# Narrow products of latent attention on whole 32-bit operands instead of split ones

## The chip, the core and the metric

The kernel runs on one core of a Trainium2 chip. A core has five engines with instruction queues of their own: TensorE (PE, the matrix engine; its weight loads are listed apart as PEld), VectorE (DVE), ScalarE (ACT), GpSimd (POOL) and SyncE (SP, which issues the transfers here). Each queue is worked in order, and the engines wait for each other through semaphores. Operands lie in an on-chip memory of 128 partitions, and matrix products land in banks of 512 32-bit words a partition. The metric is the time of one execution on the device in microseconds (us).

## The reference

A decoder trunk of two layers over 256 tokens of width 1024, all in 32-bit floats. Each layer is a half-step feed-forward part, an attention part, a second half-step feed-forward part and a gated input embedding, each followed by a layer norm. The first layer's attention is a forgetting attention; the second layer's is multi-head latent attention with 16 heads, and this is where the change lies:

```python
def scores(start):
    qn = lax.dynamic_slice_in_dim(q_nope, start, BLOCK_Q, axis=1)
    qr = lax.dynamic_slice_in_dim(q_rope, start, BLOCK_Q, axis=1)
    s = jnp.einsum('bqhd,bkhd->bhqk', qn, k_nope) + jnp.einsum('bqhr,bkr->bhqk', qr, k_rope)
    return s.astype(jnp.float32) * scale
...
    s = jnp.where(k_pos[None, :] <= q_pos[:, None], s, -jnp.inf)
    w = jax.nn.softmax(s, axis=-1).astype(v.dtype)
    return jnp.einsum('bhqk,bkhd->bqhd', w, v)
```

The attention is causal and swept over two blocks of 128 queries. The first block sees the first 128 keys alone, the second block all 256.

## The kernel before

**Split operands.** TensorE is used with a reduced 32-bit type (F32R). To keep the accuracy, every operand is split in two parts: a high part, which ScalarE makes by copying to F32R, and a low part, which VectorE makes by subtracting the high part from the original (`parts`, lines 520 to 524, for results in the product banks; `split`, lines 174 to 220, for weights that come from memory). A product is then three passes (`mm3`, lines 505 to 510): high by high, high by low, low by high. Transposes through TensorE (`transpose`, line 516) and the warm-up products of `spin` (line 489) are the only ones on whole 32-bit data.

**Weights.** `Stream` loads weights in groups into three raw buffers through SP and splits them into slots (`hl0` and so on, and lent tiles such as `qk`, `ota`, `otb`, `fs`). When a split is put into the program is decided while the program is written, from a simple count of each engine's time (`busy`, `pump`, `fill`, `ahead`). In the latent attention the turns at which `pump` may split are switched off for nearly the whole stage (`hold 1`), and the list `ORDER` (lines 48 to 75) says when splits are made: `f n` fills up to n weights ahead, `a` makes the high part of one split, `l` makes its low part.

**The latent attention** (`mla`, from line 1261). `ORDER` also fixes the order of the steps. For each head h:

- `gen h` multiplies the latents by the head's weights and leaves, in one bank, 256 columns of queries (two blocks of 128) and 256 columns of keys; `parts` splits all 512 columns into one half of the tile `qk` (even heads one half, odd heads the other).
- `QK h` makes the scores: block 0 by the first 128 keys (128 columns), block 1 by all 256 keys (256 columns). Each takes three passes on the split nope parts and two passes with the rope part (`zT` and `kr`; the trace names these `fs,xT`).
- `sm h` and `div h` do the softmax: mask and minimum on VectorE (line 1455), exponential on ScalarE (line 1460), scaling on VectorE (line 1472).
- `T h` transposes the 384 columns of probabilities in three pieces and splits them into the tile `PT`. Columns 0 to 255 belong to the first 128 keys (both query blocks), columns 256 to 383 to the second 128 keys (second query block alone).
- `AV h` multiplies by the values: three passes of 256 columns for the first 128 keys, three of 128 columns for the second 128 keys, then `parts` into an output tile. `O h t` is the output projection.

The values are made four heads at a time: `V g t` (group g of four heads, key block t) leaves a bank of 512 columns and copies its high part on ScalarE; `vlo g t` later makes the low part on VectorE and lets the bank go. Values live in a ring of five buffers named `g4`.

Scores and transposes share two banks called `tr`; `gen` and `AV` share two called `h`. `rope copy`, `rot`, `zs` and `zU` prepare the rope part of heads 8 to 15 in the early part of the stage, partly on GpSimd.

Of the kernel before, what the change touches and what calls it, by code (L numbers as in the profile page):

```python
# [10 lines left out]
F32 = mybir.dt.float32  # L11
F32R = mybir.dt.float32r
AF = mybir.ActivationFunctionType
# [409 lines left out]
class Trunk:  # L423
# [837 lines left out]
    def mla(self, li):  # L1261
        nc, S, a = self.nc, self.S, self.a
# [4 lines left out]
        v = {}  # L1267
        cqt = self.tl([128, 2, 3, 256], F32R, "gb", 1)
        cqtok = self.tl([128, 2, 768], F32, "PT", 1)
        zt = self.own([128, 2, D], F32, "ota")  # L1270
        qk = self.own([128, 2, 2, 512], F32R, "qk")

        dqb, dqr = {}, {}
# [20 lines left out]
        vps = {}  # L1294

        def V(g, t):
            w = self.use(("kvv", g))
            ps = vps[g, t] = self.bank(("h", "y", "tr")[VRING[g][t]])
            for k in range(2):
                self.mm3(  # L1300
                    ps, lambda i: self.ckv[:, i, 256 * k + 128 * t : 256 * k + 128 * t + 128],
                    lambda i: w[:, i, 512 * k : 512 * k + 512], k == 0, k == 1,
                )
            o = v[t, g] = self.tl([128, 2, 512], F32R, "g4", 5)
            nc.scalar.activation(o[:, 0, :], ps, AF.Copy)
            S.busy(act=512)
# [107 lines left out]
        st, PT = {}, {}  # L1414

        def gen(h):
            ps = self.bank("h")
            hp, s = h // 2, h % 2
            w = self.use(("kvk", hp))
            for k in range(2):  # L1420
                self.mm3(
                    ps[:, 256:512], lambda i: w[:, i, 256 * k + 128 * s : 256 * k + 128 * s + 128],
                    lambda i: self.ckv[:, i, 256 * k : 256 * k + 256], k == 0, k == 1,
                )
            w = self.use(("qn", hp))
            for k in range(3):
                self.mm3(
                    ps[:, 0:256], lambda i: w[:, i, 256 * k + 128 * s : 256 * k + 128 * s + 128],
                    lambda i: cqt[:, i, k, :], k == 0, k == 2,
                )  # L1430
            o = qk[:, h % 2]
            self.parts(o[:, 0, :], o[:, 1, :], ps)

        def QK(h):
            b = self.bank("tr")
            kr = self.kr
            o = qk[:, h % 2]
            for q0, c0, c1 in ((0, 0, 128), (128, 128, 384)):
                w = c1 - c0
                self.mm3(  # L1440
                    b[:, c0:c1], lambda i: o[:, i, q0 : q0 + 128],
                    lambda i: o[:, i, 256 : 256 + w], True, False,
                )
                for i in (0, 1 + (h % 2 if h < 8 else 1)):
                    self.mm(b[:, c0:c1], zT[:, h, q0 : q0 + 128], kr[:, i, 0:w], False, i > 0)
            st[h] = b
# [34 lines left out]
        def T(h):  # L1481
# [4 lines left out]
            o = self.tl([128, 2, 384], F32R, "PT", 1)  # L1486
            self.parts(o[:, 0, :], o[:, 1, :], b[:, 0:384])
            PT[h] = o

# [7 lines left out]
        def AV(h):  # L1497
            if h in (0, 10):
                OT.append(self.own([128, 4, 2, 256], F32R, "ota" if h else "otb"))
            o = PT.pop(h)  # L1500
            ps = self.bank("h")
            g, c = h // 4, 128 * (h % 4)
            for m, (i, jj) in enumerate(((0, 0), (0, 1), (1, 0))):
                self.mm(
                    ps[:, 0:256], v[0, g][:, i, c : c + 128], o[:, jj, 0:256], m == 0, False
                )
            for m, (i, jj) in enumerate(((0, 0), (0, 1), (1, 0))):
                self.mm(
                    ps[:, 128:256], v[1, g][:, i, c : c + 128], o[:, jj, 256:384], False, m == 2
                )  # L1510
            ot = ot_of(h)
# [107 lines left out]
```

## Time and profile before

| What | Value |
|---|---|
| Time, median of 3 runs | 1083.85 us (1083.05 to 1084.26) |
| Profiled execution, span from first to last instruction | 1080.8 us |
| Median of the runs less that span | 3.05 us |
| TensorE busy | 1065.8 us, 99% of the span |
| VectorE busy | 718.8 us, 67% |
| ScalarE busy | 543.3 us, 50% |
| Transfers over the span | 183 GB/s |

The profile gives no time of the profiled execution beside its span; what lies around the span is taken from the median of the runs. In a row of the groups, a line of the kernel, an engine and an operation are followed by the written and read tiles, the shape and the count; after the bar stand the busy time in us and the mean of one in ns, and after the second bar the idle time of the engine just before them, with what ended it. In the timeline a row begins with its start and length in us, and neighbours of one kind are merged. Matrix passes overlap in the records, so their pitch from start to start tells more than their length. A waits row gives the waiting engine and line, what ended the wait, the total in us, how often, and the longest.

### The profile page before, as it was taken

The page shows a single profiled execution, that of the slowest core. Times are in us where ns is not written, and L with a number is a line of the kernel's source. Part 1 is how long each engine was busy: PE and PEld are TensorE (multiplying, and loading weights), DVE is VectorE, ACT ScalarE, POOL GpSimd, SP SyncE. Part 2 cuts the span into 40 slices and gives each one's busy share as a digit, 9 for nine tenths or more (in the row PEclk, how much of TensorE's full clock was granted, in tenths as well). Part 3 has the DMA queues.
Part 4 walks back from the last instruction along what each step waited for, and adds up shares of the span by engine and source line. Part 5 has one row for each costly group of instructions (what it writes and reads, how often), then busy time and mean ns, then how long its engine had stood idle before and what let it go on. Part 6 is the DMA issues. An engine that isn't in the chain of part 4 may idle for free.

```text
span 1080.8 us, 17731 instructions
## 1 busy us (share of the span) xinstructions
PE 1065.8 (99%) x7210; PEld 971.2 (90%) x7210; DVE 718.8 (67%) x1042; ACT 543.3 (50%) x806; POOL 73.2 (7%) x104
## 2 busy tenths in 40 slices
PE   9999999999999999999999999999999999999996
PEld 7989999899879999998899999988899889898986
DVE  4665645888797545558966564388777886455566
ACT  4565433666646444444555443336576465444431
POOL 0000000222200000000320000012200000000000
PEclk9999999999999999999999999999999999999999
DMA  8787752653358756455588564343445568565502
GB/s 270 230 312 241 245 181 83 195 166 137 114 172 290 254 181 190 148 201 156 164 275 266 185 194 165 89 105 112 140 145 169 174 225 308 191 206 192 182 13 78
DMA packets 151428, 198.54 MB, mean 184 GB/s; under 512 B 11954, under 2 KB 130994, under 8 KB 151348
## 3 DMA queue, kind: packets, MB, share of 16 engines
q1 hardware_dynamic: 151348, 197.43, 55.8%
q8 instruction: 56, 0.92, 0.3%
q14 instruction: 24, 0.20, 0.1%
HBM read 196.35 MB, written 1.05 MB: 183 GB/s over the span
## 4 chain that ended last, share of the span: by engine, by line
PE 90%; DVE 6%; issue 2%; ACT 2%; POOL 1%; DVEq 0%; POOLq 0%; ACTq 0%
PE y L513 32%; PE h L513 32%; PE tr L513 23%; PE tr L517 2%; DVE hl L195 2%; DVE x L593 1%; ACT hl L194 1%; DVE st L575 0%; DVE x L574 0%; PE h L517 0%; DVE PT L523 0%; ACT P L1460 0%; PE tr L1100 0%; DVE g L833 0%; POOL rs L585 0%
## 5 line engine op out<-in xcount | busy, mean ns | idle before, releaser
L195 DVE TENSOR_TENSOR hl<-raw,hl 128x1024 fp32r<-128x1024 f32 (+3 forms) x276 | 321.4, 1183 | 152.0 <-ACT hl L194 150.4
L194 ACT ACTIVATE hl<-raw 128x1024 fp32r<-128x1024 f32 (+3 forms) x276 | 274.4, 1016 | 187.0 <-PE y L513 95.0
L513 PE MATMUL y<-hl,g 128*128 128x512 f32 x816 | 190.7, 390 | 0.0
L513 PEld LDWEIGHTS y<-hl,g 128*128 128x128 f32 x816 | 152.0, 188 | 30.7
L513 PE MATMUL tr<-xT,hl 128*128 128x256 f32 x1512 | 177.3, 277 | 0.0
L513 PEld LDWEIGHTS tr<-xT,hl 128*128 128x128 f32 x1512 | 174.6, 188 | 0.9 <-DVE hl L195 0.2
L513 PE MATMUL h<-xT,hl 128*128 128x256 f32 x1464 | 174.0, 278 | 0.1
L513 PEld LDWEIGHTS h<-xT,hl 128*128 128x128 f32 x1464 | 170.0, 188 | 1.5 <-DVE qk L523 0.3
L513 PE MATMUL h<-hl,xT 128*128 128x512 f32 (+2 forms) x348 | 80.9, 379 | 0.5 <-DVE xT L523 0.4
L513 PEld LDWEIGHTS h<-hl,xT 128*128 128x128 f32 x348 | 61.5, 188 | 13.0 <-DVE xT L523 0.9
L513 PE MATMUL y<-hl,xT 128*128 128x512 f32 (+3 forms) x360 | 65.4, 334 | 0.0
L513 PEld LDWEIGHTS y<-hl,xT 128*128 128x128 f32 x360 | 55.5, 188 | 6.3 <-ACT xT L522 0.4
L585 POOL TENSOR_TENSOR rs<-ve,mhalf 128x1 f32<-128x1 f32 x16 | 15.2, 952 | 601.2 <-DVE ve L584 601.2
L522 ACT ACTIVATE xT<-tr 128x512 fp32r<-128x512 f32 (+1 forms) x36 | 19.2, 550 | 57.1 <-PE tr L517 57.0
L513 PE MATMUL y<-hl,otb 128*128 128x512 f32 x168 | 43.4, 399 | 0.7 <-DVE hl L195 0.5
L523 DVE TENSOR_TENSOR g<-P,g 128x512 fp32r<-128x512 f32 x37 | 25.6, 692 | 25.8 <-ACT g L522 25.8
L522 ACT ACTIVATE g<-P 128x512 fp32r<-128x512 f32 x37 | 23.4, 632 | 32.2 <-DVE P L708 32.2
L513 PEld LDWEIGHTS y<-hl,otb 128*128 128x128 f32 x168 | 30.2, 188 | 7.2 <-DVE hl L195 0.8
L195 DVE TENSOR_TENSOR otb<-raw,otb 128x1024 fp32r<-128x1024 f32 (+1 forms) x20 | 24.1, 1202 | 16.8 <-ACT otb L194 16.8
L195 DVE TENSOR_TENSOR qk<-raw,qk 128x1024 fp32r<-128x1024 f32 (+1 forms) x21 | 25.7, 1222 | 10.8 <-ACT qk L194 10.8
L707 ACT ACTIVATE P<-tr 128x512 f32<-128x512 f32 x20 | 12.0, 598 | 40.2 <-PE tr L513 40.2
L708 DVE TENSOR_TENSOR P<-P,tr 128x512 f32<-128x512 f32 x20 | 13.8, 688 | 26.8 <-PE tr L513 15.1
(259 smaller groups left out, 1411.6 us busy)
## 6 DMA issues: line engine op xcount, KB each, us to landing
raw<-in_ffn_w_in_dram SPq DMA_DIRECT2D x170, 512.0 KB, 4.8
raw<-in_ffn_w_out_dram SPq DMA_DIRECT2D x44, 1024.0 KB, 5.0
raw<-in_fox_w_in_dram SPq DMA_DIRECT2D x11, 1024.0 KB, 5.4
raw<-in_ple_w_gate_dram SPq DMA_DIRECT2D x8, 1024.0 KB, 5.1
raw<-in_mla_w_o_dram SPq DMA_DIRECT2D x8, 1024.0 KB, 5.0
gb<-in_ln_g_dram SPq DMA_DIRECT2D x8, 512.0 KB, 6.4
gb<-in_ln_b_dram SPq DMA_DIRECT2D x8, 512.0 KB, 7.8
raw<-in_fox_w_o_dram SPq DMA_DIRECT2D x4, 1024.0 KB, 4.9
```

Of the source, the lines that this page charges most:

```text
L194: nc.scalar.activation(hi[:, c], src[:, c], AF.Copy)
L195: nc.vector.tensor_tensor(lo[:, c], src[:, c], hi[:, c].bitcast(F32), op=ALU.subtract)
L513: self.nc.tensor.matmul(out, lhsT, rhs, start=start, stop=stop)
L517: self.nc.tensor.transpose(out, in_, self.ident)
L522: self.nc.scalar.activation(hi, src, AF.Copy)
L523: self.nc.vector.tensor_tensor(lo, src, hi.bitcast(F32), op=ALU.subtract)
L585: nc.gpsimd.tensor_tensor(rs, ve, self.mhalf, op=ALU.pow)
L593: nc.vector.scalar_tensor_tensor(xs, xs, rs if i else mv[:, 0:1], self.gb[:, i, c0:c1], op0=ALU.mult if i else ALU.subtract, op1=ALU.add i ...
L707: nc.scalar.activation(gt, ps[0], AF.Silu)
L708: nc.vector.tensor_tensor(gt, gt, ps[1], op=ALU.mult)
```

## The change

Two of the four products of a head, both 128 columns wide, are made on the whole 32-bit operands, in one call each instead of three passes on the split parts: the scores of query block 0 (`QK`), and the values of the second 128 keys (`AV`).

- `gen` splits only columns 128 to 511 (384 instead of 512) and copies the first 128 queries and the first 128 keys unsplit to a raw place (one more ScalarE copy of 256 columns, read with a stride). `heads(h)` names these places. The query block 0 is no longer kept split.
- `T` splits 256 columns instead of 384 and copies the last 128 unsplit (one more ScalarE copy of 128 columns).
- `V g 1` copies its bank unsplit; the four steps `vlo g 1` are gone from `ORDER`, and nothing else of that list is changed.
- The raw places are tiles under names that earlier parts of the kernel have done with: `negc` (the raw queries and keys of even heads in columns 0 to 255, and the raw probabilities of all heads in columns 256 to 383) and `nrm` (odd heads), the latter taken in `gen 1`.

```diff
         qk = self.own([128, 2, 2, 512], F32R, "qk")
+        raws = [self.tl([128, 384], F32, "negc", 1)]
...
-            o = v[t, g] = self.tl([128, 2, 512], F32R, "g4", 5)
-            nc.scalar.activation(o[:, 0, :], ps, AF.Copy)
+            if t:
+                o = v[t, g] = self.tl([128, 512], F32, "g4", 5)
+                nc.scalar.activation(o, vps.pop((g, t)), AF.Copy)
+            else:
+                o = v[t, g] = self.tl([128, 2, 512], F32R, "g4", 5)
+                nc.scalar.activation(o[:, 0, :], ps, AF.Copy)
...
+        def heads(h):
+            return qk[:, h % 2, :, 0:384], raws[h % 2][:, 0:256]
+
         def gen(h):
...
-            o = qk[:, h % 2]
-            self.parts(o[:, 0, :], o[:, 1, :], ps)
+            if h == 1:
+                raws.append(self.tl([128, 384], F32, "nrm", 1))
+            o, raw = heads(h)
+            self.parts(o[:, 0, :], o[:, 1, :], ps[:, 128:512])
+            nc.scalar.activation(
+                raw.rearrange("p (i c) -> p i c", i=2), ps.rearrange("p (i c) -> p i c", i=2)[:, :, 0:128], AF.Copy)
+            S.busy(act=256)
 
         def QK(h):
...
-                self.mm3(
-                    b[:, c0:c1], lambda i: o[:, i, q0 : q0 + 128],
-                    lambda i: o[:, i, 256 : 256 + w], True, False,
-                )
+                if q0:
+                    self.mm3(b[:, c0:c1], lambda i: o[:, i, 0:128], lambda i: o[:, i, 128:384], True, False)
+                else:
+                    self.mm(b[:, c0:c1], raw[:, 0:128], raw[:, 128:256], True, False)
+                    S.busy(pe=128)
...
             o = self.tl([128, 2, 384], F32R, "PT", 1)
-            self.parts(o[:, 0, :], o[:, 1, :], b[:, 0:384])
-            PT[h] = o
+            raw = raws[0][:, 256:384]
+            self.parts(o[:, 0, 0:256], o[:, 1, 0:256], b[:, 0:256])
+            nc.scalar.activation(raw, b[:, 256:384], AF.Copy)
+            S.busy(act=128)
+            PT[h] = o, raw
...
-            for m, (i, jj) in enumerate(((0, 0), (0, 1), (1, 0))):
-                self.mm(
-                    ps[:, 128:256], v[1, g][:, i, c : c + 128], o[:, jj, 256:384], False, m == 2
-                )
+            self.mm(ps[:, 128:256], v[1, g][:, c : c + 128], raw, False, True)
+            S.busy(pe=128)
```

More of the change, by code (lines that the diff above doesn't have):

```diff
@@ L1436, in QK @@
             kr = self.kr
-            o = qk[:, h % 2]
+            o, raw = heads(h)
             for q0, c0, c1 in ((0, 0, 128), (128, 128, 384)):
                 w = c1 - c0
-                self.mm3(
-                    b[:, c0:c1], lambda i: o[:, i, q0 : q0 + 128],
-                    lambda i: o[:, i, 256 : 256 + w], True, False,
-                )
+                if q0:
[3 more added lines that the diff above has]
+                    S.busy(pe=128)
                 for i in (0, 1 + (h % 2 if h < 8 else 1)):
@@ L1499, in AV @@
                 OT.append(self.own([128, 4, 2, 256], F32R, "ota" if h else "otb"))
-            o = PT.pop(h)
+            o, raw = PT.pop(h)
             ps = self.bank("h")
```

8 rows, old and new, of the table ORDER are left out of this document.

## The prediction

> **What bounds the kernel now.** I read the page first (busy time by engine, the chain that ended last), then the groups by line and shape, then the timeline of the attention stage.
>
> ```profile
> span 1080.8 us, 17731 instructions
> PE 1065.8 (99%) x7210; PEld 971.2 (90%) x7210; DVE 718.8 (67%) x1042; ACT 543.3 (50%) x806; POOL 73.2 (7%) x104
> PE 90%; DVE 6%; issue 2%; ACT 2%; POOL 1%; DVEq 0%; POOLq 0%; ACTq 0%
> ```
>
> TensorE (PE) is busy 99% of the span and is 90% of the last chain. Work taken off PE shortens the run, except where PE was going to wait anyway. The next view gives those waits between 690 and 880 us, around the attention stage, and the one after 850 us.
>
> ```profile
> PE h L513 <- DVE hl L195: 1.6, 2, 1.0
> PE tr L517 <- ACT qk L522: 1.1, 1, 1.1
> PE y L513 <- DVE hl L195: 0.5, 1, 0.5
> PE h L513 <- DVE PT L523: 0.4, 1, 0.4
> PE tr L517 <- DVE P L1472: 0.4, 1, 0.4
> ```
>
> ```profile
> PE tr L517 <- DVE x L593: 0.2, 1, 0.2
> ```
>
> So about 4 us of waiting in the stage, nearly all for a weight split or a probability on VectorE (DVE). By stretches (columns: length; busy PE, PEld, DVE, ACT, POOL with counts; granted clock; DMA share; GB/s) it lies early:
>
> ```profile
> 740.00:760.00 20.00, 16.51 (x116) 14.56 (x115) 16.71 (x33) 11.48 (x25) 10.82 (x9) 1.00 0.28 86
> 760.00:780.00 20.00, 19.91 (x130) 17.72 (x130) 14.47 (x38) 12.91 (x33) 2.10 (x2) 1.00 0.46 139
> 800.00:820.00 20.00, 20.00 (x142) 18.61 (x141) 16.16 (x39) 13.27 (x31) 0.00 (x0) 1.00 0.52 165
> ```
>
> From 760 us PE has no room left, and a saved PE nanosecond counts in full; from 740 to 760 us others set the pace. The granted clock is 1.00 throughout.
>
> **The products.** Here is the first head's scores step, its passes merged by kind: three of 128 columns on the split nope parts, two of 128 with the rope part, then three and two of 256, then the next head.
>
> ```profile
> 741.01 0.45 PE L513 MATMUL tr<-qk 128*128 128x128 f32 x3
> 741.30 0.39 PE L513 MATMUL tr<-fs,xT 128*128 128x128 f32 x2
> 741.52 0.57 PE L513 MATMUL tr<-qk 128*128 128x256 f32 x3
> 741.92 0.40 PE L513 MATMUL tr<-fs,xT 128*128 128x256 f32 x2
> 742.16 0.45 PE L513 MATMUL tr<-qk 128*128 128x128 f32 x3
> ```
>
> From start to start the ten passes take 742.16 - 741.01 = 1.15 us, 0.115 each, although five of them stream half as many columns. A 128-column pass is thus not cheaper than a 256-column one: within 1.15 us the rope pair of 256 takes 0.24, so 0.120 each. Each pass brings its own weight load, and a narrow pass is held to the pitch of these. Removing a pass saves a slot, some 0.11 us.
>
> The only products on whole 32-bit operands in this trace are the warm-up ones of line 493, 384 columns wide. The second-last and last of their matrix records (merged, then the last alone), the load beside the former, and from the page a load of split operands:
>
> ```profile
> 5.64 0.81 PE L493 MATMUL y<-mask 128*128 128x384 f32 x2
> 5.96 0.49 PE L493 MATMUL y<-mask 128*128 128x384 f32 x1
> 5.64 0.19 PEld L493 LDWEIGHTS y<-mask 128*128 128x128 f32 x1
> ...
> L513 PEld LDWEIGHTS y<-hl,g 128*128 128x128 f32 x816 | 152.0, 188 | 30.7
> ```
>
> The program has four such products and the trace eight records of line 493, so one product is two load-and-pass pairs. The pitch is 5.96 - 5.64 = 0.32 us per record, 0.83 ns per column; scaled to 128 columns that is 0.107 us a record. Its load starts together with a pass (5.64 and 5.64) and takes 0.19, like the 188 ns of split operands, so I take it as hidden: a record costs one slot, between 0.107 (the scaled stream) and 0.120 (the rope pair). A whole product is two slots, 0.21 to 0.24 us; three split passes are three, 0.11 to 0.115 each. The saving is 0.09 to 0.13 per product; I take 0.108, nearest to the two pitches in the scores step itself. There are 16 heads with one product in the scores and one in the values: 32 x 0.108 = **3.5 us** off PE. These groups confirm the number, 48 passes each, three a head:
>
> ```profile
> L513 PE MATMUL tr<-qk 128*128 128x128 f32 x48 | 7.9, 274 | 0.0
> L513 PE MATMUL h<-PT,g 128*128 128x128 f32 x48 | 7.1, 257 | 0.0
> ```
>
> [...]
>
> **What it costs on ScalarE and VectorE.** Per head, one copy each is added, and the split pairs get narrower.
>
> ```profile
> L522 ACT ACTIVATE qk<-h 128x512 fp32r<-128x512 f32 x15 | 9.0, 602 | 10.2 <-PE h L513 10.2
> L522 ACT ACTIVATE PT<-tr 128x384 fp32r<-128x384 f32 x16 | 7.9, 493 | 2.0 <-PE tr L517 1.9
> L522 ACT ACTIVATE otb<-h 128x256 fp32r<-128x256 f32 x10 | 3.8, 382 | 0.4 <-PE h L513 0.2
> L523 DVE TENSOR_TENSOR qk<-h,qk 128x512 fp32r<-128x512 f32 x16 | 11.0, 687 | 9.1 <-ACT qk L522 9.0
> L523 DVE TENSOR_TENSOR PT<-tr,PT 128x384 fp32r<-128x384 f32 x16 | 8.8, 549 | 0.3 <-ACT PT L522 0.2
> L523 DVE TENSOR_TENSOR otb<-h,otb 128x256 fp32r<-128x256 f32 x10 | 4.2, 415 | 0.3 <-ACT otb L522 0.3
> L1310 DVE TENSOR_TENSOR g<-tr,g 128x512 fp32r<-128x512 f32 x3 | 2.1, 686 | 0.3 <-ACT g L1305 0.3
> ```
>
> ScalarE in `gen`: 602 becomes 493 (384 columns) + 382 (the raw 256): +0.27 us. In `T`: 493 becomes 382 + 0.27 (128 columns, by the slope (602 - 382)/256 = 0.86 ns): +0.16. Over 16 heads +6.9 us on an engine that is busy 13 of 20 us here. VectorE: `gen` -0.14, `T` -0.13, sixteen times -4.4, and four `vlo` of 0.69 go: -7.1 us in all. No DMA, POOL or SP instruction is added or moved. The cover of the new copies is PE's own backlog: VectorE's low part (549 ns) starts with the raw copy (382 ns) and ends after it, and scores and values read both. Without that cover each copy costs PE its 0.16 to 0.27.
>
> **Where the cover is thin.** Three places.
>
> ```profile
> 739.22 1.19 ACT L1391 ACTIVATE xT<-tr 64x512 fp32r<-64x512 f32 x2
> 740.43 1.41 DVE L1393 TENSOR_TENSOR xT<-tr,xT 64x512 fp32r<-64x512 f32 x2 [0.39 <-ACT xT L1391]
> 747.70 0.30 PE L517 MATMUL tr<-ident,P 128*128 128x128 f32 x1 [1.06 <-ACT qk L522]
> 751.19 1.05 ACT L194 ACTIVATE hl<-raw 128x1024 fp32r<-128x1024 f32 x1
> 752.27 1.22 DVE L195 TENSOR_TENSOR hl<-raw,hl 128x1024 fp32r<-128x1024 f32 x1 [0.26 <-ACT hl L194]
> 759.75 1.10 PE L513 MATMUL h<-gb,hl 128*128 128x256 f32 x7 [0.98 <-DVE hl L195]
> 834.53 1.82 PE L513 MATMUL y<-hl,ota 128*128 128x512 f32 x6
> 847.28 0.79 PE L513 MATMUL h<-PT,g 128*128 128x256 f32 x5 [0.39 <-DVE PT L523]
> ```
>
> First, behind `gen 1` ScalarE has the rope parts (739.22) on which VectorE's next steps wait, and those lead to the first probabilities (747.70); behind `gen 3` it has the split at 751.19, on which VectorE's queue up to the wait at 759.75 hangs. Each comes some 0.2 later (+0.27 less what overlaps), 0.1 is given back by a narrower `T`: **+0.3 us**. Second, the six products ahead of that wait (scores 0 to 3, values 0 and 1) only lengthen waits: 6 x 0.108 = **0.65 us** of the 3.5 is not had. Third, at 834.53 PE waits for a value part queued on ScalarE behind `gen 15` (+0.2), and for the last two heads VectorE sets the pace, so that some four products' gain is lost (0.43), while narrower `T` parts let these waits end 0.32 sooner (0.13 on VectorE for each of two, the rest on ScalarE): together **+0.1 us**; the 0.2 falls into the same waits and is not counted twice.
>
> The removed `vlo` steps free VectorE at 748 and later, where no PE wait of the stage hangs on it, and a PSUM bank 0.7 us sooner; I cost them at nothing, with the gain bounded in a rival. The program's own planner now counts two narrow passes for three and may shift weight splits of the later feed-forward part by one step; PE waits for nothing but 0.2 us after 850, so zero. The scores' first product no longer gives the planner a turn; splitting on such turns is switched off in this stretch.
>
> Sum: -3.5 + 0.65 + 0.3 + 0.1 = **-2.45 us**. Against the profiled execution: span 1080.8 to 1078.35. The median of the runs, 1083.85, is 3.05 above that span, taken as unchanged: **1081.4 us**. No change that a measurement can tell means within 0.2%, 2.2 us.
>
> **Rivals.** (a) *The loads are not hidden*, the other side. If a whole-operand load cannot run beside the pass before it, each record costs load and stream: 0.111 + 0.107 = 0.218 us, a product 0.436 against 0.338, +3.1 us; less six products in waits (-0.6), plus 0.4: 1086.8. It decides once a record takes more than 0.169. For it: the pitch of two loads this close, 0.107, isn't in the trace (the nearest is 0.32). Against: the load at 5.64 lies beside the pass at 5.64 and the pitch leaves no gap; split loads do the same at 0.115. [...]
>
> (b) *ScalarE becomes late.* If a third of its 6.9 us reaches PE, the 2.45 are gone: 1083.8. For it: ScalarE's queue is in order, and copies stand ahead of splits. Against: it sits idle 10.2 us ahead of the `qk` group above, waiting for PE.
>
> (c) *VectorE's relief pays.* Half of the 3.6 us of waits at 747 to 760 go as well: 1079.6. For it: 7.1 us less on the engine that these waits name. Against: the two chains above start on ScalarE.
>
> (d) *A borrowed tile couples steps.* Raw scores and raw probabilities share one tile. Were order kept by whole tile, the scores of heads 2, 4, 6 and 10, right behind a `T`, would wait for its copies: 0.38 + 0.27 each, 2.6 us, so 1084.0. Against it, scores of head 12 read one half of `qk` while ScalarE writes the other:
>
> ```profile
> 822.12 0.45 PE L513 MATMUL tr<-qk 128*128 128x128 f32 x3
> 822.32 0.60 ACT L522 ACTIVATE qk<-h 128x512 fp32r<-128x512 f32 x1 [0.30 <-PE h L513]
> ```
>
> **How the numbers follow.** Forecast 0.48 (own range 1080.4 to 1082.4), (c) 0.14, (b) 0.18, (a) 0.13, (d) 0.07. Forecast and (c) give faster, but a seventh of the forecast's own range is within 0.2%: 0.55. Same: that seventh, (b) for the most part, half of (d): 0.25. Slower: (a), the rest of (b) and (d): 0.20. The range 1079.2 to 1085.0 holds the forecast, (b), (c) and (d) and leaves out (a) and some tails.
>
> **What the new profile would show.** Two records a head on the raw tiles in each of scores and values, pitch 0.107 to 0.12; the scores step about 1.04 us for nine slots; PE full from 760; the wait at 759.75 ending as late as now or 0.3 later. A record pitch over 0.169, new PE waits naming ScalarE after 760, or missing waits before it would make me wrong, in the sense of (a), (b), (c).

## The result, and the profile after

The changed kernel takes 1092.18 us (median of 4 runs, 1090.81 to 1094.78) against 1084.05 us for the kernel before beside it (1083.05 to 1084.57): a ratio of 1.0075, 95% interval 1.0062 to 1.0087. It is 8.1 us slower, where 2.45 us less was forecast. The profiled execution has a span of 1089.0 us, 8.2 more than that of before.

The page of the changed kernel: its span, busy time by engine, and the chain that ended last.

```profile
span 1089.0 us, 17695 instructions
...
PE 1066.7 (98%) x7178; PEld 968.8 (89%) x7178; DVE 713.5 (66%) x1038; ACT 548.0 (50%) x838; POOL 72.6 (7%) x104
...
PE 81%; DVE 8%; ACT 4%; issue 2%; DMA 2%; SPq 1%; POOL 1%; DVEq 0%; ACTq 0%; POOLq 0%
```

PE has the 32 instructions fewer that the change promised, VectorE is 5.3 us less busy and ScalarE 4.7 us more (-7.1 and +6.9 were forecast; the next instruction of an engine can start some 0.1 us before the one ahead of it has ended, as 829.29 + 0.38 and 829.57 below, and the busy time counts that once, which may be the difference). None of these is 8 us, and no engine is near a bound that it was not near before. What is new is that PE's part of the last chain fell from 90% to 81%: the time went into waiting.

What TensorE waited for most between 690 and 880 us, in the changed kernel (microseconds in all, times, the longest):

```profile
PE h L513 <- DVE hl L195: 1.7, 2, 1.0
PE tr L517 <- DVE P L1486: 1.6, 2, 1.3
PE h L513 <- ACT PT L522: 1.5, 1, 1.5
PE tr L513 <- ACT negc L1503: 1.2, 2, 0.7
PE y L513 <- ACT otb L522: 1.2, 2, 0.9
PE tr L517 <- DVE x L593: 1.1, 2, 0.9
PE y L513 <- ACT ota L522: 1.0, 1, 1.0
```

Four of the seven rows name ScalarE (ACT), 4.9 us together; before, one row did, with 1.1. By stretches (columns as in the forecast):

```profile
760.00:780.00 20.00, 18.85 (x116) 17.03 (x117) 13.87 (x35) 11.28 (x32) 4.44 (x3) 0.91 0.54 166
...
800.00:820.00 20.00, 18.90 (x119) 16.20 (x118) 14.89 (x38) 13.79 (x36) 0.00 (x0) 1.00 0.66 210
820.00:840.00 20.00, 17.93 (x128) 15.99 (x127) 13.12 (x36) 11.34 (x31) 0.00 (x0) 1.00 0.35 117
```

The last of these stretches in the kernel before:

```profile
820.00:840.00 20.00, 19.88 (x146) 18.30 (x145) 15.47 (x41) 12.54 (x31) 0.00 (x0) 1.00 0.48 160
```

Between 800 and 820 us PE was busy 20.00 of 20 us before; now it is 18.90, and in the next stretch 17.93 instead of 19.88. PE's backlog, which was to cover the new copies, is gone. From 760 to 780 the granted clock is 0.91 and was 1.00.

What stands behind it is in the waits of ScalarE itself, between 735 and 860 us:

```profile
ACT negc L1503 <- DVE PT L523: 9.7, 16, 1.3
ACT nrm L1443 <- DVE qk L523: 8.7, 8, 1.7
ACT negc L1443 <- DVE qk L523: 7.8, 8, 1.4
```

The three rows are the 32 new raw copies: 16 of `T` (line 1503), 16 of `gen` (line 1443). Every one of them waited, and every time for VectorE's low part of the same product, 26.2 us in all. The copy needs nothing of what the low part writes. Both only read the same bank of PSUM, the memory of the product banks. The timeline shows how exact this is, and what hangs on it; here are the low part and the copy of `gen 0` and, further down, rows around the values of head 11 (start, duration, engine, line; in brackets the idle time ahead of it and who ended it):

```profile
738.59 0.56 DVE L523 TENSOR_TENSOR qk<-h,qk 128x384 fp32r<-128x384 f32 x1
739.18 0.39 ACT L1443 ACTIVATE negc<-h 128x256 f32<-128x256 f32 x1 [1.41 <-DVE qk L523]
...
827.84 0.95 DVE L195 TENSOR_TENSOR hl<-raw,hl 128x768 fp32r<-128x768 f32 x1
828.71 0.55 DVE L523 TENSOR_TENSOR qk<-h,qk 128x384 fp32r<-128x384 f32 x1
829.29 0.38 ACT L1443 ACTIVATE nrm<-h 128x256 f32<-128x256 f32 x1 [1.70 <-DVE qk L523]
829.57 1.05 ACT L207 ACTIVATE hl<-raw 128x1024 fp32r<-128x1024 f32 x1
830.52 0.38 ACT L522 ACTIVATE PT<-tr 128x256 fp32r<-128x256 f32 x1
830.93 0.42 DVE L523 TENSOR_TENSOR PT<-tr,PT 128x256 fp32r<-128x256 f32 x1 [1.67 <-ACT PT L522]
830.95 0.96 PE L513 MATMUL h<-PT,g 128*128 128x256 f32 x3 [1.47 <-ACT PT L522]
831.38 0.28 ACT L1503 ACTIVATE negc<-tr 128x128 f32<-128x128 f32 x1 [0.49 <-DVE PT L523]
```

The low part ends at 738.59 + 0.56 = 739.15 and the copy starts at 739.18. At 828 us the low part itself stands behind a weight split on VectorE (827.84), so ScalarE stands still for 1.70 us. Behind the copy in ScalarE's queue are a weight split (829.57) and the high part of the transposed probabilities (830.52), and PE, whose next pass needs the latter, waits 1.47 us for it. The last row is the same order in `T`: the low part reads columns 0 to 255 of the bank and ends at 831.35, the copy reads columns 256 to 383 and starts at 831.38. Disjoint columns did not help in any of the 16 heads. All 32 copies start 0.03 to 0.04 us after the low part of their bank has ended.

PE also waits for a copy itself (1.2 us, `negc L1503` above). The longer of the two waits ends at 817.33, with passes that need nothing of the copy but write a bank of the same pair (`tr`); the copy ends at 817.00 + 0.28 = 817.28, so the bank seems to have come free only when the copy had read it.

What holds the copy back is not in the rows: they show who ended each wait, VectorE's low part, 32 times of 32. That the shared bank is the reason is an estimate from the same rows, since the two instructions have no tile but that bank in common. The prediction did not weigh it.

To follow where the time goes, the table gives how much later than in the trace of before the same pass of PE starts (the first 256-column pass of each step, in `gen` the first that reads `gb`; microseconds; the last row is the span). Four columns belong to experiments described below.

| step | changed | `raw_first` | `before_copies_last` | `before_copies_first` | `late_heads` |
|---|---|---|---|---|---|
| `gen 0` | +0.36 | +0.61 | +0.56 | +1.38 | +1.24 |
| `gen 4` | +2.37 | +0.85 | +3.76 | +3.09 | +1.23 |
| values 2 | +3.53 | +2.00 | +3.76 | +4.24 | +1.20 |
| scores 8 | +3.13 | +1.01 | +6.82 | +4.24 | +0.41 |
| values 11 | +5.95 | -0.05 | +11.69 | +4.24 | -0.65 |
| values 15 | +7.27 | -0.48 | +14.74 | +4.86 | -1.08 |
| end | +8.18 | -0.57 | +14.72 | +4.90 | -1.04 |

The changed kernel loses 2.0 us from `gen 0` to `gen 4`, 1.2 to the values of head 2 (at the reduced clock), gains 0.4 up to the scores of head 8, and from there loses 4.1 until the values of head 15, and 0.9 more at the layer norm behind the stage. The 0.36 is there at 690 us already, ahead of all code that was changed; such differences ahead of the stage (up to 2.7 us, in `late_gb`) are why verdicts go by the medians and their intervals. The trace of before is moreover one of its faster executions: its span is 1080.8 us, and the 21 executions of that kernel beside `raw_first` have a median span of 1082.4.

### The profile page after: what moved, and what is told of

It reads as the page before. It is cut to its first block, busy times and chain, and to the rows that moved or that the text cites. A ratio compares the mean times of both kernels' runs of the same rounds, so it can differ in the third digit from the quotient of the medians.

```text
span 1089.0 us, 17695 instructions
## 1 busy us (share of the span) xinstructions
PE 1066.7 (98%) x7178; PEld 968.8 (89%) x7178; DVE 713.5 (66%) x1038; ACT 548.0 (50%) x838; POOL 72.6 (7%) x104
## 4 chain that ended last, share of the span: by engine, by line
PE 81%; DVE 8%; ACT 4%; issue 2%; DMA 2%; SPq 1%; POOL 1%; DVEq 0%; ACTq 0%; POOLq 0%
PE y L513 29%; PE h L513 29%; PE tr L513 21%; DVE hl L195 3%; PE tr L517 1%; ACT hl L194 1%; ACT P L1474 1%; SPq L348 1%; DMA gb<-in_ln_b_dram 1%; DVE x L593 1%; DVE PT L523 1%; DMA raw<-in_mla_w_uq_dram 1%; ACT hl L207 1%; DMA raw<-in_ffn_w_in_dram 0%; DVE qk L523 0%
```

## The experiments

The theory, formed from the lines above: each copy waits for VectorE's low part because both read one bank, and what stands behind it in ScalarE's queue comes late (the order theory). Its rivals: the copies cost by their own 6.9 us of ScalarE, wherever they stand (the work theory, the forecast's rival b); or the products on whole operands are dearer than three split passes (the forecast's rival a).

**The copy ahead of the split.** The change stays whole; only the order of two statements is turned, in `gen` and in `T`. Then the high part follows the copy on ScalarE, and VectorE's low part, which needs the high part anyway, waits for no other engine than it did.

```diff
-            self.parts(o[:, 0, :], o[:, 1, :], ps[:, 128:512])
             nc.scalar.activation(
                 raw.rearrange("p (i c) -> p i c", i=2), ps.rearrange("p (i c) -> p i c", i=2)[:, :, 0:128], AF.Copy)
+            self.parts(o[:, 0, :], o[:, 1, :], ps[:, 128:512])
...
-            self.parts(o[:, 0, 0:256], o[:, 1, 0:256], b[:, 0:256])
             nc.scalar.activation(raw, b[:, 256:384], AF.Copy)
+            self.parts(o[:, 0, 0:256], o[:, 1, 0:256], b[:, 0:256])
```

> Only the place of the raw copies changes: each stands ahead of the split of the same bank on ScalarE, so no copy can wait for VectorE's low part. Theory 'wait' (the 26 us in which ScalarE stood still ahead of its raw copies, until VectorE had read the same bank, are what held TensorE up): those waits are gone, the 11 us of new TensorE stalls go with them, and the time falls to 1080 to 1084. Rival 'load' (the 32 copies themselves, 10.6 us of ScalarE time, are what made it late): the copies are all still there and the high parts come 0.28 to 0.38 later, so 1090 or more. Rival 'clock' (the stretch of half clock at 763 to 766 is the main loss): about 2 us come back, 1090.

Measured: 1082.29 us (1081.33 to 1085.61, 11 runs), before 1084.56, ratio 0.9988 (0.9979 to 0.9996). Turning two statements is worth 9.9 us. The same stretches of this kernel:

```profile
800.00:820.00 20.00, 20.00 (x139) 18.52 (x138) 14.69 (x39) 14.45 (x37) 0.00 (x0) 1.00 0.60 189
820.00:840.00 20.00, 19.77 (x140) 17.96 (x140) 15.15 (x41) 13.45 (x40) 0.00 (x0) 1.00 0.48 159
```

PE is full again with ScalarE busier (14.45 us against 13.79 in the changed kernel). In the timeline, the copy in `gen 1` now starts when PE delivers, and the high part follows at its heels:

```profile
739.34 0.38 ACT L1442 ACTIVATE nrm<-h 128x256 f32<-128x256 f32 x1 [1.03 <-PE h L513]
739.62 0.49 ACT L522 ACTIVATE qk<-h 128x384 fp32r<-128x384 f32 x1
```

**The copy between high and low part.** The pair of `parts` is written out, with the copy in the middle. Now it is VectorE that waits for the copy.

```diff
-            self.parts(o[:, 0, :], o[:, 1, :], ps[:, 128:512])
+            nc.scalar.activation(o[:, 0, :], ps[:, 128:512], AF.Copy)
             nc.scalar.activation(
                 raw.rearrange("p (i c) -> p i c", i=2), ps.rearrange("p (i c) -> p i c", i=2)[:, :, 0:128], AF.Copy)
+            nc.vector.tensor_tensor(o[:, 1, :], ps[:, 128:512], o[:, 0, :].bitcast(F32), op=ALU.subtract)
+            S.pair(384)
```

(and the same in `T`)

> Each raw copy stands between ScalarE's high part and VectorE's low part. ScalarE never waits for VectorE here; the low part waits for the raw copy instead, 0.29 us in gen and 0.18 in T. Theory 'wait': 1080 to 1084, within 1 us of the kernel with the copies first, because it is ScalarE's standing still that costs and not the order in itself. Rival 'load': 1090 or more, as in that kernel. If the low part's delay on VectorE matters as much as ScalarE's, this one is the slower of the two by 2 us or more.

Measured: 1082.84 us (1080.86 to 1085.77), ratio 0.9987 (0.9978 to 0.9996): the same as `raw_first` within what can be told. VectorE's waits in this kernel, between 735 and 860 us:

```profile
DVE qk L1445 <- ACT negc L1443: 6.5, 4, 1.7
DVE qk L1445 <- ACT nrm L1443: 5.7, 4, 2.6
```

The wait stands on the other side of the pair now, 12.2 us in `gen` altogether, and costs nothing that can be measured: VectorE had waited for the high part before (9.0 us ahead of the `qk` group, and 11.6 in `raw_first`), and the copy adds 0.38 us at most. So it is not a wait between the two readers as such that costs, but ScalarE standing still with other work behind it.

**The copies alone.** The kernel before, with the 32 copies added and read by nobody, behind the split as in the change (the diff shows this one) or ahead of it, with the copy above the call of `parts`. The products stay on split operands.

```diff
+            raw = raws[h % 2][:, 0:256]
             self.parts(o[:, 0, :], o[:, 1, :], ps)
+            nc.scalar.activation(
+                raw.rearrange("p (i c) -> p i c", i=2), ps.rearrange("p (i c) -> p i c", i=2)[:, :, 0:128], AF.Copy)
...
+            raw = raws[0][:, 256:384]
             self.parts(o[:, 0, :], o[:, 1, :], b[:, 0:384])
+            nc.scalar.activation(raw, b[:, 256:384], AF.Copy)
```

> The kernel before, with all its split products, and the 32 raw copies added behind the split of the same bank, as in the changed kernel; nothing reads them. Theory 'wait': the copies alone bring the loss: ScalarE waits some 26 us for VectorE ahead of them (low parts are 128 columns wider, so rather 28), and the time is 1093 to 1098, that is the changed kernel's loss plus the gain of the products that is now missing. Rival 'products' (whole-operand products or their operands' lateness cause the loss): with the products as before nothing waits for the copies, 1084 to 1086.

> The same, with the copies ahead of the split. ScalarE has the same added work (10.6 us) without a wait for VectorE. Theory 'wait': 1084 to 1087, the price of the copies' own time alone. Rival 'load': as slow as with the copies last, 1092 or more.

Measured: copies behind the split 1097.45 us (1097.32 to 1097.71), ratio 1.0126 (1.0112 to 1.0140); copies ahead 1087.53 us (1087.36 to 1088.06), half a microsecond above the range expected, ratio 1.0035 (1.0022 to 1.0047). ScalarE's waits with the copies behind the split:

```profile
ACT negc L1495 <- DVE PT L523: 10.0, 15, 1.0
ACT nrm L1437 <- DVE qk L523: 9.8, 8, 1.7
ACT negc L1437 <- DVE qk L523: 8.6, 8, 2.0
```

The same waits come up in a kernel that has none of the new products: 31 of the 32 lie in this window, 28.4 us, and the last ends at 862. Four kernels now make a square, medians in microseconds:

| | copies ahead | copies behind the split | difference |
|---|---|---|---|
| split products, copies unread | 1087.53 | 1097.45 | 9.9 |
| whole products | 1082.29 | 1092.18 | 9.9 |
| difference | -5.2 | -5.3 | |

The order costs 9.9 us whichever products are used, and the rest of the change (products, narrower parts, four `vlo` gone) gives 5.2 whichever order. (The kernels before beside them lie between 1084.05 and 1084.56, so the square is good to about half a microsecond, and each entry may hold a chance term of 1.2 us, described with the clock below.) The copies themselves, ahead, cost 1087.53 - 1084.56 = 3.0 us. The table of positions says where, for one trace: 1.71 us from `gen 0` to `gen 4`, 1.15 from there to the values of head 2, at half clock, nothing from there to the values of head 11 (+4.24 and +4.24), and 0.62 from there to those of head 15. So the work theory holds where PE has no backlog, at the start of the stage and a little at its end; in between the same copies are free.

**Half the order.** Only one of the two places has its copy behind the split: `gen` in the one kernel, `T` in the other. The edits are those of `raw_first`, made in the other place only.

> Of the two raw copies only that of gen stands behind the split of its bank, as in the changed kernel; that of T stands ahead. ScalarE waited 16.5 us ahead of the copies of gen and 9.7 us ahead of those of T. If the loss goes with the length of these waits, gen brings 63% of the 9.9 us between the two placements: about 1088.5. If it goes with what is queued behind the copy, gen is the dearer one still, since a weight split's high part follows it on ScalarE in most heads: 1089 to 1090.

> The other way round: only the copy of T stands behind its split. By the length of the waits 37% of 9.9 us: about 1086. If it is only gen that matters: 1082 to 1083.

Measured: `gen_last` 1090.96 us (1088.98 to 1092.0, before 1084.54), ratio 1.0059 (1.0045 to 1.0073); `t_last` 1083.89 us (1082.84 to 1087.81), ratio 1.0003 (0.9992 to 1.0014). Neither fell into a range expected: the one is slower than 1090, the other lies between 1083 and 1086. ScalarE's waits between 735 and 860 us, first in `gen_last`, then in `t_last`, and last the exponentials' row of `raw_first`:

```profile
ACT P L1474 <- DVE nm L1469: 15.2, 15, 2.6
ACT nrm L1443 <- DVE qk L523: 8.7, 8, 1.7
ACT negc L1443 <- DVE qk L523: 8.0, 8, 1.4
```

```profile
ACT negc L1503 <- DVE PT L523: 13.6, 16, 1.4
ACT P L1474 <- DVE nm L1469: 7.2, 9, 2.6
```

```profile
ACT P L1474 <- DVE nm L1469: 17.1, 15, 2.6
```

Against `raw_first` the 16.7 us that ScalarE stands in `gen` cost 8.7 us by the medians, and the 13.6 us in `T` cost 1.6. The rows tell a part of the reason: the exponentials (`P`) wait for the row maximum `nm` of VectorE, 17.1 us in `raw_first`. With `T`'s copies behind the split that falls to 7.2, so that 9.9 of the 13.6 us replace waiting that was there anyway; with `gen`'s it falls to 15.2 only. Behind `T`'s copy in ScalarE's queue stand seven exponentials and seven weight splits, behind `gen`'s copy three weight splits, not most as was expected, and nine times of 16 the copy or high part of transposed probabilities, like those that PE waited for at 830.95 in the changed kernel. That the price follows from these is argued, not shown by a run of its own. At the values of head 15, `t_last` is 1.37 us ahead of the kernel before, as good as `raw_first`. By its trace what it lost came behind the stage, at the wait for the gain and bias of the layer norm; but this trace is of the fastest of its ten executions (1082.84), and doesn't show what the slower ones lost.

**The copies on VectorE.** As in the changed kernel, behind the split, but both copies made by the engine that makes the low part.

```diff
-            nc.scalar.activation(
-                raw.rearrange("p (i c) -> p i c", i=2), ps.rearrange("p (i c) -> p i c", i=2)[:, :, 0:128], AF.Copy)
+            nc.vector.tensor_copy(
+                raw.rearrange("p (i c) -> p i c", i=2), ps.rearrange("p (i c) -> p i c", i=2)[:, :, 0:128])
...
-            nc.scalar.activation(raw, b[:, 256:384], AF.Copy)
+            nc.vector.tensor_copy(raw, b[:, 256:384])
```

> The changed kernel as it is, but both raw copies are made by VectorE, behind its own low part in its own queue. No ScalarE instruction waits for a low part any more; ScalarE has less work than before the change, VectorE 3.9 us more than before (32 copies of some 0.41 and 0.28 us, 11.0, less 7.1). Theory 'wait': 1082 to 1086, much nearer to the copies-first kernel than to the changed one. Rival 'products late' (scores and values wait for operands that come last, whoever copies them): 1089 or more, as the copies still come behind the low part.

Measured: 1082.59 us (1082.14 to 1084.36, before 1084.33), ratio 0.9985 (0.9975 to 0.9994). Low part and copy are in one queue here, and none of the seven longest rows of ScalarE's waits between 735 and 860 us (0.9 us and more) ends with a low part, as 26.2 us of them did in the changed kernel. The longest of ScalarE's waits in this kernel:

```profile
ACT P L1474 <- DVE nm L1469: 26.8, 15, 3.0
```

ScalarE is busy less than in the changed kernel (73.2 against 79.3 of the 125 us from 735 to 860) and idles more, but ahead of exponentials that wait for VectorE's row maximum. VectorE, 720.7 us busy against 713.5, carries the copies nearly as well as ScalarE does ahead of the split: the copies as such fit on either engine.

**Only where PE has a backlog.** `raw_first` gives +0.24 us up to `gen 4` and -2.48 from the values of head 2 to those of head 15. So heads 0 to 3 keep the products of before (with `vlo 0 1` put back), heads 4 to 15 have the whole operands, copies ahead.

```diff
+            if h < 4:
+                o = qk[:, h % 2]
+                self.parts(o[:, 0, :], o[:, 1, :], ps)
+                return
...
+                if h < 4:
+                    self.mm3(b[:, c0:c1], lambda i: o[:, i, q0 : q0 + 128], lambda i: o[:, i, 256 : 256 + w], True, False)
+                elif q0:
...
-            if t:
+            if t and g:
                 o = v[t, g] = self.tl([128, 512], F32, "g4", 5)
```

> Copies ahead of the splits, and whole-operand products only for heads 4 to 15; heads 0 to 3 as in the kernel before. In the kernel with the copies ahead, TensorE was 2.0 us later than before at the values of head 2 and then won 2.5 us over the next 26 products. Theory 'early copies': the 2.0 us come from copies in a stretch where ScalarE and VectorE set the pace (0.9) and from half clock behind the longer wait (1.1); without them the first 24 products' gain is had in full: span 2.2 to 2.5 us under that of before, time about 1082 and 0.2% under before. Rival: the half clock falls where it will, whatever the early copies do; then it is 1083, no better than with copies in all heads.

Measured: 1081.69 us (1080.11 to 1083.0, 11 runs, before 1084.54), ratio 0.9975 (0.9966 to 0.9984). This version beats both kernels. That it beats `raw_first` too isn't shown: the two differ by 0.6 us and the intervals overlap. As to the half clock the rival is right: it came in `late_gb` too, which has no early copies either (below). Its scores step of head 4 is the one to hold against that of the forecast:

```profile
769.56 0.39 PE L513 MATMUL tr<-negc 128*128 128x128 f32 x2
769.70 0.42 PE L513 MATMUL tr<-fs,xT 128*128 128x128 f32 x2
769.96 0.57 PE L513 MATMUL tr<-qk 128*128 128x256 f32 x3
770.36 0.40 PE L513 MATMUL tr<-fs,xT 128*128 128x256 f32 x2
770.60 2.91 PE L513 MATMUL y<-hl,otb 128*128 128x512 f32 x12
```

From 769.56 to 770.60 it is 1.04 us, nine slots where there were ten in 1.15. A whole-operand product takes two records, and the step is 0.11 us shorter. That strikes out the theory of dear products. From the values of head 2 to those of head 15 the table gives 1.20 + 1.08 = 2.28 us gained, with 23 products between the two marks (12 of scores, and the values of heads 4 to 14): 0.099 each. In `raw_first` it is 2.48 us and 25 products, 0.099 as well.

**One kind of product alone.** The scores' products on whole operands and the values' as before, and the reverse, copies ahead in both.

> Whole operands for the scores of the first query block alone, copies ahead of the split; values and transposes as before. One slot of 0.10 us less in 16 products, 1.6 us, of which 4 lie in the early stretch, so 1.2 us; the gen copies cost 0.5 to 0.9 us there and perhaps the half clock of 1.1: 1083.5 to 1085.5, no difference that can be told. If products of the scores gained more than one slot each, under 1082.

> Whole operands for the values of the second 128 keys alone, copies ahead of the split in T; gen and the scores as before. Together with the kernel for the scores alone this splits the gain. One slot of 0.10 us in 16 products, of which 2 or 3 lie where others set the pace, and four low parts of values less on VectorE: 1.3 us less, 1083.0 to 1083.8; T's copies cost less in the early stretch than gen's, so 0.5 us better than the kernel with the scores alone where they differ.

Measured: scores only 1083.65 us (1081.97 to 1085.46, before 1084.54), ratio 0.9993 (0.9984 to 1.0002); values only 1083.13 us (1081.34 to 1084.01, before 1084.33), ratio 0.9989 (0.9980 to 0.9998). The gains, 0.9 and 1.2 us, add up to 2.1; both together (`raw_first`) gave 2.3. Neither kind carries the gain alone, and nothing speaks for a coupling between them. The intervals are wider than the difference of the two, and that of the scores alone includes no gain at all.

**The layer norm's loads.** In the changed kernel the layer norm behind the stage waits for the loads of gain and bias, which stand in SyncE's queue behind four weight loads. Here are the load of the gain and its reader in the timeline:

```profile
848.39 7.26 SPq L348 DMA_DIRECT2D raw<-in_ffn_w_in_dram  x4
855.69 0.51 SPq L445 DMA_DIRECT2D gb<-in_ln_g_dram  x1
...
862.75 0.75 DVE L593 SCALAR_TENSOR_TENSOR x<-x,mv,gb 128x512 f32<-128x512 f32 x1 [0.67 <-DMA gb<-in_ln_g_dram]
```

In `late_heads` these loads are moved to right behind `gen 15`:

```diff
-    "O 11 0", "f 4", "f 2", "f 4", "a", "QK 14", "gen 15", "AV 12", "T 13", "sm 14", "f 1", "div 14 0", "l",
+    "O 11 0", "f 4", "f 2", "f 4", "a", "QK 14", "gen 15", "gb", "AV 12", "T 13", "sm 14", "f 1", "div 14 0", "l",
...
-    "div 15 0", "l", "AV 14", "O 7 1", "hold 0", "O 8 1", "hold 1", "f 3", "gb", "f 1", "T 15", "O 9 1",
+    "div 15 0", "l", "AV 14", "O 7 1", "hold 0", "O 8 1", "hold 1", "f 3", "f 1", "T 15", "O 9 1",
```

> The kernel with whole-operand products from head 4 on and the copies ahead, with one more edit: the two loads of the layer norm's gain and bias are put into the queue of transfers right behind gen 15, ahead of four loads of feed-forward weights that they stood behind. In the runs so far they landed at 853 to 856 us, when the norm needs them; in the kernel with the copies between they landed 8.3 us after issue and 1.5 us of gain were lost there. Theory 'gb': they land about 7 us sooner, the 0.5 us that TensorE waits for the norm's output shrink, and executions in which a load lands late no longer lose up to 1.5 us: 1080.5 to 1081.7. Rival: the weight loads behind them come later and feed-forward products wait: 1082.5 or more.

Measured: 1081.75 us (1080.36 to 1084.09, before 1084.33), ratio 0.9972 (0.9961 to 0.9983), the same as `late_heads`. The loads are issued 11 us sooner by the traces (835.37 against 846.76) and the norm no longer waits for them, and it buys nothing that can be measured: in `late_heads` PE waits 0.5 us at that place in all, here 0.3.

## Why the prediction was wrong

**The step that failed** is the cover of the new copies: "VectorE's low part (549 ns) starts with the raw copy (382 ns) and ends after it". The two do not start together; the copy starts when the low part has ended, 32 times of 32. I had taken two readers of one bank on two engines as independent, because neither writes what the other reads. The rows of before that I had looked at could not show it: a low part (line 523) there follows the high part (line 522) of the same bank, whose result it needs anyway. A wait that no row shows should at least have been priced. The forecast's own rows, 549 and 415 ns for the narrower low parts, give 16 x (0.549 + 0.415) = 15.4 us of ScalarE as a first estimate; the measured 26.2 is more, because a low part can itself be late, as at 828 us behind a weight split.

**What it was worth.** 9.9 us, by the square. Without it, the forecast has the right sign and about the right size: `raw_first`, which is the change with the order that the forecast assumed, is 2.27 us faster than before by the medians (0.4 to 2.3 by the interval of the ratio), where 2.45 was forecast. A part of that is luck, as the terms did not all come out: the trace of `raw_first` holds 1.15 us at half clock that no term stands for. From `gen 0` to the end of the program it gains 0.61 + 0.57 = 1.18 us with these in it, 2.33 without.

**Point by point.**

- The product: three slots become two. Right: the record's pitch (0.116 us a slot over the nine of the step), the scores step (1.04 us forecast and measured) and the loads being hidden, by the same 1.04 us. The 0.108 a product measured 0.099, so 3.2 us for 32 and not 3.5. The group row of the values' whole products in the changed kernel shows two records a head:

```profile
L513 PE MATMUL h<-negc,g 128*128 128x128 f32 x32 | 6.3, 279 | 0.0
```

- Rival (a), loads not hidden: wrong for the same reason; the time that it would have given, 1086.8, lies nearer to the result than the forecast does, but not by its mechanism.
- Early thin cover, +0.3 us up to the wait at 759.75: in `raw_first` it is 0.85 - 0.61 = 0.24 us. In the changed kernel it is 2.0. Right for the work, not for the order.
- ScalarE, rival (b): the right engine, and the wrong mechanism and size. It was priced at a third of 6.9 us, the copies' own work. That work costs 3.0 us in the kernel before with copies ahead; the wait costs 9.9 more. The argument against (b), that ScalarE "sits idle 10.2 us ahead of the `qk` group", says nothing about a stop in the middle of its queue: idle time ahead of one instruction isn't slack for those behind another. The sign that the prediction named for (b), new PE waits that name ScalarE after 760, did come.
- VectorE's relief, rival (c): the 5.2 us that the rest of the change gives, on top of the copies, is more than 32 products at 0.099 to 0.108 (3.2 to 3.5). The remainder of some 2 us may be narrower splits, fewer `vlo` or the clock's chance term; it was not taken apart. No gain of this kind showed in the forecast's place, the waits at 747 to 760: the changed kernel and `raw_first` are not earlier than before at `gen 4`.
- Borrowed tile, rival (d): wrong by the changed kernel's trace. The scores of heads 2, 4, 6 and 10 read their half of `negc` at 752.95, 771.77, 786.73 and 814.04 us, and the copy of the `T` ahead of them in the program writes the same tile only at 757.31, 775.30, 789.17 and 817.00. Order was not kept by whole tile in these four heads.
- Zero for the loads: not quite. The gain and bias loads come late at the end of the stage in the changed kernel (0.9 us in PE's longest wait there, and 0.9 between values 15 and the end in the table). They did so in three of the traces, and the forecast had called PE free of waits from there.
- The clock at 1.00 throughout: wrong in some executions, see below.
- The 3.05 us between span and median: not what lies around the span. In the executions for which both are on record, time less span is 2.1 to 2.2 us for the kernel before and 1.8 for the changed one; the rest came from a profiled execution that was faster than the median. The forecast of the difference does not hang on it.

**Still open.** How the 5.2 us divide between PE's slots and the relief of VectorE. Whether the wait could be removed with ScalarE's copy left behind the split: by the author's estimate that would need a second bank, and it was not tried. And so it is not shown by a run that the bank is what orders the two readers; the runs show that the second in the program waits for the first, on ScalarE in the changed kernel (32 times, 26.2 us) and on VectorE in `raw_between` (8 times in `gen`, 12.2 us).

## What to carry to other kernels

Two readers of one PSUM bank on two engines ran one after the other here, in program order, and those of `T` on disjoint columns (32 copies of 32); before adding a reader, ask which engine stands still for it and what is queued behind it, and let the same engine read twice, ahead of the handover (1092.18 became 1082.29 us by turning two statements). The length of such a wait isn't its price: 13.6 us, of which exponentials gave back 9.9 by waiting less, cost under 2; 16.7 us, of which they gave back 1.9, cost over 8. And where PE has no backlog yet, it may be better to leave the step as it was: the same change came out 0.6 us better (1081.69 against 1082.29, with overlapping intervals) when the first four heads were left out.

## What the runs showed that was not expected

**A half clock.** The changed kernel's trace around 760 us, one microsecond a row (columns as before; the number ahead of the last two is the granted clock):

```profile
759.00:760.00 1.00, 0.46 (x4) 0.25 (x3) 1.00 (x1) 0.36 (x1) 0.92 (x2) 1.00 0.30 92
760.00:761.00 1.00, 0.84 (x6) 0.77 (x6) 1.00 (x2) 0.00 (x0) 1.00 (x1) 1.00 0.81 217
761.00:762.00 1.00, 0.13 (x2) 0.00 (x0) 1.00 (x2) 0.63 (x1) 1.00 (x2) 1.00 0.93 244
762.00:763.00 1.00, 0.88 (x5) 0.88 (x6) 0.82 (x5) 0.11 (x1) 1.00 (x1) 0.68 0.36 103
763.00:764.00 1.00, 1.00 (x5) 0.93 (x5) 0.16 (x1) 1.00 (x6) 1.00 (x2) 0.50 0.70 106
...
765.00:766.00 1.00, 1.00 (x5) 0.71 (x4) 1.00 (x2) 0.41 (x2) 0.00 (x0) 0.62 1.00 414
```

PE was busy 1.43 of the three microseconds from 759 to 762, in two waits for weight splits (the first row of PE's waits above, 1.7 us, which the kernel before has too with 1.6), and then ran at half clock for 0.64 + 1 + 1 + 0.76 = 3.4 us (the row left out, 764 to 765, has 0.50 as well; a granted clock of 0.68 over a microsecond is 0.64 of it at half). From `gen 4` to the values of head 2 that cost 3.53 - 2.37 = 1.16 us, and 1.15 in `raw_first` and `before_copies_first`. The next rows are of the stretch from 760 to 765 us, of `late_gb` and then of `late_heads`, whose programs for PE are the same up to there:

```profile
760.00:765.00 5.00, 3.53 (x17) 3.04 (x18) 3.95 (x9) 2.42 (x7) 4.76 (x3) 0.81 0.76 196
```

```profile
760.00:765.00 5.00, 3.94 (x21) 3.13 (x22) 3.95 (x10) 3.80 (x10) 3.32 (x3) 1.00 0.85 262
```

The one lost 1.2 us there and the other none (the table's +1.23 and +1.20). PE's load ahead of it was the same in both, with waits of 0.60 and 0.98 us. So in these two traces it came by chance of the moment, and whoever compares single traces of such a kernel carries a term of 1.2 us. Eight of the thirteen traces of this case hold one such stretch: two between 740 and 760 us, five that begin between 759 and 764, and one, in `before_copies_last`, outside 740 to 775, where its granted clock is 1.00. The changed kernel's is 3.41 us long; in `raw_first` a granted clock of 0.66 over the 5 us from 760 makes 3.4, in `late_gb` 0.81 and 0.85 over the two stretches of 5 us from there 3.4 as well. The mean granted clock over the span is 0.996 or 0.997 in these eight and 0.998 or 0.999 in the other five.

What brings it on is not shown. The two gaps just ahead of it in the changed kernel are 0.70 and 0.99 us long (the waits for weight splits that end at 760.16 and 762.12). That three microseconds half idle (1.43 us busy) can be enough is an estimate from that trace alone, and `gen_last`, with PE busy 3.23 of the 5 us from 760, had a granted clock of 1.00 over them.

**A wait that the change does not show.** No changed line of the kernel says that the copy depends on the low part: the two write different tiles and read, in `T`, different columns. It shows in the rows of ScalarE's waits (26.2 us in the changed kernel); in the text of the kernel nothing hints at it but that two engines read one bank.
